# SwiGLU's Winograd products in the order P5, P6, P7, P4, P3, small gate loads on the weights' queue, half the first operands by VectorE

## The chip, the cores and the metric

One core of a Trainium2 chip runs the whole program. The metric is the device time of one execution in microseconds. Five engines work side by side, each through its own queue and in its own order: TensorE (matmul and transposes), VectorE, ScalarE, GpSimd, and SyncE, which here does nothing but issue DMAs. ScalarE issues DMAs too, between its computing instructions.

## The reference, cut to what matters

```python
h = modulate(rms_norm(x, g_pre_mix), shift, scale)      # x: 512 tokens, ctx: 256, width 2048
u, v, q, k, vv, g, d_f, d_b = split_proj(h @ w_in)      # the context too
la = log_sigmoid(d @ wd2 + bd) / 16                     # GLA's decay gates; wd2 is 16 x 512
mixed = einsum('hij,bnjhd->bnihd', w_s, layer_norm(gelu(v))) + b_s   # spatial gating
y = concatenate([u * mixed, gla_out]) @ w_out           # 1024 + 1024 columns
x = x + gate * rms_norm(y)
a, b = split(modulate(rms_norm(x), ...) @ w_ffn_in)     # 2048 -> 2 x 5632
x = x + gate2 * rms_norm((silu(a) * b) @ w_ffn_out)
```

All tensors are float32.

## The kernel before

Every float32 matmul operand is split into a high and a low part (`hi`, a rounded copy made by ScalarE, and `lo`, the rest, by VectorE), and `three` multiplies hi x hi, hi x lo and lo x hi. Names that end in h and l are such parts. Work that is not urgent comes from generators that two pumps step once per weight tile: `bg` (spatial gating, residual, operand preparation) and `bgm` (the modulation vectors).

**Context projections.** The weights of the context's keys (`ck`) and values (`cv`) come tile by tile through SyncE's queue (`ckr`, `cvr`, three buffers). TensorE multiplies them while `bg` runs the spatial gating: `wsr` is loaded, transposed (`wsp`), multiplied into `cb`, and eight heads follow, each with `mx` on TensorE, the load `ul` of the gate operand, `mt` on VectorE and the store `a_dr`, both DMAs on SyncE. `wdc` is the low-rank weight whose product `cd` runs beside `ck`; ScalarE casts it. Two tiles `wd2` for the decay gates are cleared by GpSimd and then filled by twelve DMAs of 1 KB to 16 KB (L673, L674). They are used only after the context projections.

**First operands of the FFN.** The normalised tokens are transposed by TensorE into PSUM, 256 columns at a time, and `h2_pair` scales and shifts them into `h2f` (L1141). `half` 0 serves the first two token tiles; `make_top` asks for eight pairs of it, j = 0 and 1 each. `s_parts` casts them into operands S1 and S2; S3 to S7 come later, from `make_rest`. The residual of the second half (`residual`) runs between them: a norm over VectorE and ScalarE, then new scaled rows `yo`.

**SwiGLU.** The product with `w_ffn_in` runs by 2 x 2 blocks with seven products instead of eight (Strassen-Winograd). Eleven groups of 512 hidden columns each take P1 to P7; one product is 48 matmuls of 512 columns in four quarters q. A quarter loads one 128x1024 block of weights (SyncE, four buffers `R`), sums it with the running chain `X` where the product wants a sum, and casts (`parts`): P5 adds block (0,1), P6 adds (1,1), P4 adds (1,0). After these come P3 and P7 in turn: z is block (1,1), and y is (0,1) plus z. Products leave PSUM through 128x512 sums by VectorE (`vtt`, L1202): `u`, `u4` (printed w), `a1` (printed g). [...] Groups 0 to 5 have their P1 and P2 made earlier, partly between the groups. `turn_hidden` transposes a finished group and stores it to DRAM; `hidden` loads it back (`gr`, R buffers) and casts it into `gh`, `gl` for the last projection `fo`. In the last group eight of those parts are made ahead of P7 and P3, and P3 loads its blocks again (`v`).

Of the kernel before, what the change touches and what calls it, by code (L numbers as in the profile page):

```python
# [14 lines left out]
AF = mybir.ActivationFunctionType  # L15
ALU = mybir.AluOpType
# [9 lines left out]
HID = 5632  # L26
# [67 lines left out]
def trunk_kernel(ctx, tc, cmat, cmask, x, c, ctxt, c_ctx, w_mod, b_mod, g_pre_mix, g_post_mix, g_pre_ffn,  # L94
                 g_post_ffn, w_in, ln_g, ln_b, w_s, b_s, wd2_f, bd_f, wd2_b, bd_b, out_g, w_out, w_ffn_in,
                 w_ffn_out, out):
    nc = tc.nc
    V, S, T, G = nc.vector, nc.scalar, nc.tensor, nc.gpsimd
# [12 lines left out]
    def bank(name, main=True):  # L111
        return pm.tile([P, 512], F32, tag="mm" if main else "ms", bufs=6 if main else 2, name=name)

    def slot(name, dt=F32, shape=(P, 512)):
        return s2.tile(list(shape), dt, tag="s2", bufs=NS, name=name)
# [177 lines left out]
    def pump():  # L293
        bg.step()
        bgm.step()
# [14 lines left out]
    def three(o, a, b, start, stop, lhs_first=True):  # L310

        mm(o, a[0], b[0], start, False)
        mm(o, a[0], b[1], False, False)
        mm(o, a[1], b[0], False, stop)

    def cut(pair, lo, n):
        return pair[0][:, lo:lo + n], pair[1][:, lo:lo + n]
# [35 lines left out]
    def turn(o, tok, k, diag=None):  # L353

        for i in range(len(tok)):
            src = tok[i][k // 4][:, (k % 4) * P:(k % 4 + 1) * P]
            if diag is None:
                T.transpose(o[:, i * P:(i + 1) * P], src, ident)
            else:
                mm(o[:, i * P:(i + 1) * P], src, diag[:, i, :], True, True)  # L360
# [5 lines left out]
    fmodA = cp.tile([P, KT], F32, name="fmodA")  # L366
    fmodB = cp.tile([P, KT], F32, name="fmodB")
# [139 lines left out]
    for ka, kb in ((0, 4), (4, 8), (8, KT)):  # L507
        first, last = ka == 0, kb == KT
# [154 lines left out]
    bgm.drain()  # L663


    wd2 = [slot(f"wd2{g}") for g in range(2)]
    for g in range(2):
        G.memset(wd2[g][:65, :], 0.0)
        w4 = wd2[g].rearrange("p (h d c) -> p h d c", h=2, d=2)
        for d_, (w, b_) in enumerate(((wd2_f, bd_f), (wd2_b, bd_b))):  # L670
            src = w[0][:, g * 256:(g + 1) * 256].rearrange("r (h c) -> r h c", h=2)
            for r in (0, 32):
                nc.scalar.dma_start(w4[r + 16 * d_:r + 16 * d_ + 16, :, d_, :], src)  # L673
            nc.scalar.dma_start(w4[64:65, :, d_, :],  # L674
                                b_[0:1, g * 256:(g + 1) * 256].rearrange("r (h c) -> r h c", h=2))


    def mods_ffn_in():
        for k0 in range(0, KT, 4):
            yield from mod_ab(3 * D, k0, 4, cx, gpf, fmodA, fmodB, "mf", mod_bg, late=1)  # L680
# [18 lines left out]
    def turn_ck(i):  # L699

        ps = bank(f"ckx{i}", False)
        for j in range(2):
            h = 2 * i + j
            for t in range(NC):
                T.transpose(ps[:, j * CTX + t * P:j * CTX + (t + 1) * P], ckt[t][:, h * P:(h + 1) * P], ident)
        S.copy(ckT[i], ps)

    cvacc = [[bank(f"cv{t}_{g}") for g in range(2)] for t in range(NC)]
    for k, ws in stream(w_in[0], OVV, 1024, KT, "cv"):
# [17 lines left out]
    for o in (0, 512):  # L727
        n = min(512, len(LEVELS) * P - o)
# [290 lines left out]
    def raw2(name):  # L1019
        return st2.tile([P, 1024], F32, tag="R", bufs=4, name=name)  # L1020

    def parts(src, name):

        wh = st2.tile([P, 1024], F32R, tag="wh", bufs=3, name=name + "h")
        wl = st2.tile([P, 1024], F32R, tag="wl", bufs=3, name=name + "l")
        S.copy(wh, src)
        V.tensor_tensor(out=wl, in0=src, in1=wh.bitcast(F32), op=ALU.subtract)
        return wh, wl

    def wide(w, r, c0, t, name):  # L1030

        load(t.rearrange("p (k c) -> p k c", k=2), w[r:r + 2 * P, c0:c0 + 512].rearrange("(k p) c -> p k c", p=P))
        return t
# [90 lines left out]
    NQ = KT // 4  # L1124
# [8 lines left out]
    def h2_pair(half, k0):  # L1133

        ps = bank(f"h2p{half}_{k0}", False)
        tmp = slot(f"h2f{half}_{k0}")
        for j in range(2):
            k = k0 + j
            c = slice(j * 256, (j + 1) * 256)
            turn(ps[:, c], yo[half * 2:half * 2 + 2], k)  # L1140
            S.activation(tmp[:, c], ps[:, c], AF.Identity, bias=fmodB[:, k:k + 1], scale=fmodA[:, k:k + 1])  # L1141
        return tmp

    top = [[None] * NQ for _ in range(2)]
# [41 lines left out]
    def product(p, q, accs, wp, nq):  # L1186
        hi, lo = SP[p][q]
        for j in range(2):
            for t in range(2):
                c = slice(j * 256 + t * P, j * 256 + (t + 1) * P)  # L1190
                three(accs[t], (hi[:, c], lo[:, c]), cut(wp, j * 512, 512), q == 0 and j == 0, q == nq - 1 and j == 1)

    def two(name):
        return [bank(f"{name}{t}") for t in range(2)]
# [5 lines left out]
    def vtt(out, a, b, op):  # L1200
        for i in range(2):
            V.tensor_tensor(out=out[i], in0=a[i], in1=b[i], op=op)  # L1202

    def blk(gi, i, j, q, t):

        return wide(w_ffn_in[0], i * (D // 2) + 2 * q * P, (gi * 512, HID + gi * 512)[j], t, f"f{gi}")
# [30 lines left out]
    def hidden(k0, nk):  # L1237

        for k in range(k0, k0 + nk, 2):
            r = raw2(f"gr{k}")  # L1240
            nc.sync.dma_start(r.rearrange("p (k c) -> p k c", k=2), g_dr[k:k + 2].rearrange("k p c -> p k c"))
            for j in range(2):
                hi, lo = slot(f"gh{k + j}", F32R), slot(f"gl{k + j}", F32R)
                S.copy(hi, r[:, j * 512:(j + 1) * 512])  # L1244
                V.tensor_tensor(out=lo, in0=r[:, j * 512:(j + 1) * 512], in1=hi.bitcast(F32), op=ALU.subtract)  # L1245
                yield (hi, lo)
# [22 lines left out]
    gT, src = [], hidden(0, 20)  # L1269

    def ffn_group(gi):
        n = f"f{gi}"
        if gi not in early:
            u, X = ffn_top(gi, chain_tile)
            a1 = ffn_top2(gi, u)
        else:
            X = [blk(gi, 0, 0, q, chain_tile(f"{n}X{q}")) for q in range(NQ)]
            u, a1 = early[gi] if gi < 2 else (kept(gi, 0, "r"), kept(gi, 2, "r"))

        p5 = two(n + "p5")  # L1280
        for q in range(NQ):
            r = blk(gi, 0, 1, q, raw2(f"{n}c{q}"))
            V.tensor_tensor(out=X[q], in0=X[q], in1=r, op=ALU.add)
            product(5, q, p5, parts(X[q], f"{n}c{q}"), NQ)
            pump()
        turn_hidden()
        p6 = two(n + "p6")
        for q in range(NQ):
            r = blk(gi, 1, 1, q, raw2(f"{n}d{q}"))
            V.tensor_tensor(out=X[q], in0=X[q], in1=r, op=ALU.add)  # L1290
            product(6, q, p6, parts(X[q], f"{n}d{q}"), NQ)
            pump()
        vtt(u, u, p6, ALU.subtract)
        u4 = [fslot(f"{n}w{t}") for t in range(2)]
        vtt(u4, p5, u, ALU.add)
        p4 = two(n + "p4")
        for q in range(NQ):
            r = blk(gi, 1, 0, q, raw2(f"{n}e{q}"))
            V.tensor_tensor(out=X[q], in0=X[q], in1=r, op=ALU.add)
            product(4, q, p4, parts(X[q], f"{n}e{q}"), NQ)  # L1300
            pump()
        vtt(u, p4, u, ALU.add)
        if gi == HID // 512 - 1:
            for _ in range(8):
                gT.append(next(src))

        p7, p3 = two(n + "p7"), two(n + "p3")
        last = gi == HID // 512 - 1
        for q in range(NQ):
            z = blk(gi, 1, 1, q, raw2(f"{n}z{q}"))  # L1310
            y = blk(gi, 0, 1, q, raw2(f"{n}y{q}"))
            if not last:
                product(3, q, p3, parts(z, f"{n}z{q}"), NQ)
                pump()
            V.tensor_tensor(out=y, in0=y, in1=z, op=ALU.add)
            product(7, q, p7, parts(y, f"{n}y{q}"), NQ)
        vtt(u, u, p7, ALU.subtract)
        for t in range(2):
            S.activation(u[t], u[t], AF.Silu)
        vtt(p7, p7, u4, ALU.subtract)  # L1320
        if last:
            vtt(u, u, p7, ALU.mult)
            for q in range(NQ):
                z = blk(gi, 1, 1, q, raw2(f"{n}v{q}"))
                product(3, q, p3, parts(z, f"{n}v{q}"), NQ)
                pump()
        vtt(u4, p3, u4, ALU.subtract)
        vtt(a1, a1, u4, ALU.mult)
        if not last:
            vtt(u, u, p7, ALU.mult)  # L1330
        behind.append((gi, a1 + u))

    behind = []
# [45 lines left out]
    for ci, (k1, nk) in enumerate(((0, 20), (20, 20))):  # L1379
        if ci:  # L1380
            gT, src = [], hidden(k1, nk)
# [22 lines left out]
    gT = list(hidden(HID // P - LAST, LAST))  # L1404
# [4 lines left out]
    for t in range(NT):  # L1409
# [5 lines left out]
        for cg in range(4):  # L1415
            ps = bank(f"fz{t}{cg}")
            for k in range(LAST):
                three(ps, cut(gT[k], t * P, P), wl_[cg * LAST + k], k == 0, k == LAST - 1)
            f = facc[t][cg]
# [4 lines left out]
        r = rstd_exp(fss, 1, f"er{t}")  # L1424
# [32 lines left out]
```

## Time and profile before

| | |
|---|---|
| median of three runs | 2322.54 us (2322.45, 2322.54, 2324.78) |
| the profiled execution | 2318.14 us, of which the span 2314.9 us |
| granted TensorE clock over the span | 0.993 |
| TensorE busy | 2251.0 us, 97% |
| VectorE busy | 1597.7 us, 69% |
| ScalarE busy | 986.8 us, 43% |
| DMA traffic | 496.16 MB, 214 GB/s over the span |

The profile is of one execution. Its time is the span of the engines' records and 3.2 us around it. Busy times say how much of the span an engine worked, not which engine the others waited for; the rows further down come from single stretches of the trace. The granted clock is a share of 2.4 GHz.

### The profile page before, as it was taken

Reading aid. Unit: us, or ns where it says so; the run is one execution under the profiler, and the core shown is the slowest. Engines: PE = TensorE matmul, PEld = TensorE weight load, DVE = VectorE, ACT = ScalarE, POOL = GpSimd, SP = SyncE. Lnnn points to the kernel's source line nnn. Section 1 sums busy time; section 2 is a strip of 40 time slices with the busy share of each in tenths; the row PEclk is TensorE's granted clock in tenths of the full one; section 3 lists DMA queues with packets and bytes.
Section 4 is the critical chain, followed back from the end, with each engine's and each line's share of the span. In section 5 each row is a group of like instructions: output and inputs, shape, how many; then the busy total and the mean of one; then the engine's idle time right before and its main releaser. Section 6 shows DMA issues by size and latency. Waiting matters only on the chain.

```text
span 2314.9 us, 27795 instructions
## 1 busy us (share of the span) xinstructions
PE 2251.0 (97%) x10298; PEld 1829.1 (79%) x10298; DVE 1597.7 (69%) x2072; ACT 986.8 (43%) x1517; POOL 15.5 (1%) x25
## 2 busy tenths in 40 slices
PE   7999998999999999999999999999999999999998
PEld 2778887888878777777888788888888788888886
DVE  3886586687796565797878887788788643354346
ACT  4444334465564325864444444444445322241232
POOL 0000000000000000000000000000000000000000
PEclk9999999999999999999999999999999999999999
DMA  9966787854462686777687776676566754464344
GB/s 322 338 221 223 244 294 243 298 178 128 146 198 87 231 276 237 227 221 246 215 282 263 264 256 198 191 225 195 183 215 207 243 191 146 139 228 161 122 135 157
DMA packets 262391, 496.16 MB, mean 214 GB/s; under 512 B 22128, under 2 KB 33872, under 8 KB 262256
## 3 DMA queue, kind: packets, MB, share of 16 engines
q1 hardware_dynamic: 248960, 472.47, 62.5%
q10 hardware_dynamic: 13296, 21.94, 2.7%
q8 instruction: 80, 1.31, 0.2%
q14 instruction: 55, 0.45, 0.1%
HBM read 466.01 MB, written 28.32 MB: 214 GB/s over the span
## 4 chain that ended last, share of the span: by engine, by line
PE 76%; DMA 10%; DVE 9%; ACT 3%; issue 2%; SPq 0%; ACTq 0%; DVEq 0%
PE fo L118 16%; PE wo L118 3%; PE f8p L118 3%; PE f1p L118 3%; PE f7p L118 3%; PE f9p L118 3%; PE f6p L118 3%; PE f5p L118 3%; PE f3p L118 2%; PE f0p L118 2%; PE f4p L118 2%; PE vv1a L118 2%; PE v0a L118 2%; PE u1a L118 2%; PE fz L118 2%; PE cv L118 2%
## 5 line engine op out<-in xcount | busy, mean ns | idle before, releaser
L1245 DVE TENSOR_TENSOR gl<-gr,gh 128x512 fp32r<-128x512 f32 x44 | 28.9, 688 | 26.5 <-ACT gh L1244 26.4
L1244 ACT CAST gh<-gr 128x512 fp32r<-128x512 f32 x44 | 25.3, 618 | 47.9 <-DMA gr<-g_dr 41.0
L229 DVE SCALAR_TENSOR_TENSOR m53acc<-m53w,cpair,m53acc 128x512 f32<-128x512 f32 x16 | 12.0, 750 | 28.5 <-DMA m53w<-in_w_mod_dram 28.5
L229 DVE SCALAR_TENSOR_TENSOR m21acc<-m21w,cpair,m21acc 128x1024 f32<-128x1024 f32 x16 | 20.5, 1283 | 14.7 <-DMA m21w<-in_w_mod_dram 14.7
L862 ACT ACTIVATE lv<-lv 128x1024 f32<-128x1024 f32 x20 | 21.0, 1056 | 22.5 <-DVE lv L861 22.5
L229 DVE SCALAR_TENSOR_TENSOR m20acc<-m20w,cpair,m20acc 128x1024 f32<-128x1024 f32 x16 | 20.5, 1283 | 12.8 <-DMA m20w<-in_w_mod_dram 12.6
L118 PE MATMUL g1a<-hxh,g_0h 128*128 128x512 f32 x64 | 27.1, 423 | 0.3 <-ACT g_0h L289 0.3
L1421 ACT ACTIVATE junk<-fc 128x512 bf16<-128x512 f32 x16 | 10.1, 631 | 40.4 <-DVE fc L1420 40.3
L118 PEld LDWEIGHTS s<-lv 128*128 128x128 f32 x192 | 25.0, 191 | 2.7 <-PE g1a L118 0.7
L118 PE MATMUL vv0a<-vv_0h,hxh 128*128 128x512 f32 x64 | 26.8, 419 | 0.0
L118 PE MATMUL g0a<-hxh,g_0h 128*128 128x512 f32 x64 | 26.8, 419 | 0.0
L118 PE MATMUL vv1a<-vv_0h,hxh 128*128 128x512 f32 x64 | 26.3, 426 | 0.0
L118 PE MATMUL v1a<-v_0h,hxh 128*128 128x512 f32 x64 | 26.3, 411 | 0.0
L229 DVE SCALAR_TENSOR_TENSOR mc4acc<-mc4w,cpair,mc4acc 128x1024 f32<-128x1024 f32 x16 | 20.5, 1284 | 8.3 <-DMA mc4w<-in_w_mod_dram 8.1
L118 PE MATMUL fo<-fo_0h,gh 128*128 128x512 f32 x64 | 25.4, 397 | 0.6 <-DVE fc L1400 0.6
L118 PE MATMUL v1a<-v_0l,hxh 128*128 128x512 f32 x64 | 26.0, 406 | 0.0
L118 PE MATMUL s<-lv 128*128 128x128 f32 x192 | 25.6, 275 | 0.3 <-DVE lv L863 0.3
L118 PE MATMUL g0a<-hxh,g_0l 128*128 128x512 f32 x64 | 25.8, 403 | 0.0
L118 PE MATMUL fo<-fo_12h,gh 128*128 128x512 f32 x64 | 25.7, 402 | 0.0
L118 PE MATMUL v1a<-v_0h,hxl 128*128 128x512 f32 x64 | 25.6, 400 | 0.0
L118 PE MATMUL vv0a<-vv_0l,hxh 128*128 128x512 f32 x64 | 25.5, 399 | 0.0
L118 PE MATMUL vv1a<-vv_0l,hxh 128*128 128x512 f32 x64 | 25.4, 397 | 0.0
(3919 smaller groups left out, 7841.8 us busy)
## 6 DMA issues: line engine op xcount, KB each, us to landing
fo_r<-in_w_ffn_out_dram SPq DMA_DIRECT2D x80, 512.0 KB
gr<-g_dr SPq DMA_DIRECT2D x22, 512.0 KB
mx4w<-in_w_mod_dram SPq DMA_DIRECT2D x16, 512.0 KB
mx8w<-in_w_mod_dram SPq DMA_DIRECT2D x16, 512.0 KB
mx12w<-in_w_mod_dram SPq DMA_DIRECT2D x16, 512.0 KB
mc4w<-in_w_mod_dram SPq DMA_DIRECT2D x16, 512.0 KB
mc8w<-in_w_mod_dram SPq DMA_DIRECT2D x16, 512.0 KB
mc12w<-in_w_mod_dram SPq DMA_DIRECT2D x16, 512.0 KB
```

The costliest lines, as they stand in the source:

```text
L118: return T.matmul(o, lhsT=l, rhs=r, start=start, stop=stop)
L229: ins = V.scalar_tensor_tensor(out=acc, in0=raw[:, j].rearrange("p i c -> p (i c)"), scalar=cvec[:, k0 + j:k0 + j + 1], in1=acc, op0=ALU.m ...
L862: S.activation(lv, lv, AF.Exp)
L1244: S.copy(hi, r[:, j * 512:(j + 1) * 512])
L1245: V.tensor_tensor(out=lo, in0=r[:, j * 512:(j + 1) * 512], in1=hi.bitcast(F32), op=ALU.subtract)
L1421: S.activation(junk, f, AF.Square, accum_out=fss[:, cg:cg + 1])
```

## The change

There are three edits. The twelve wd2 loads move from ScalarE's queue, ahead of the context projections, to SyncE's queue, behind `ck`'s loop. In `h2_pair`, VectorE does the scaling of j = 1 for half 0. In `ffn_group`, P7 follows P6 and takes X minus a fresh load of block (0,0), then P4, and P3 comes last with no sum; the second SwiGLU factor's last subtraction comes after P3. In the last group, four gT parts (two gr loads) are asked for in P3's quarters in place of eight ahead of P7.

```diff
-    wd2 = [slot(f"wd2{g}") for g in range(2)]
-                nc.scalar.dma_start(w4[r + 16 * d_:r + 16 * d_ + 16, :, d_, :], src)
-            nc.scalar.dma_start(w4[64:65, :, d_, :],
+    wd2 = [slot(f"wd2{g}") for g in range(2)]
+                nc.sync.dma_start(w4[r + 16 * d_:r + 16 * d_ + 16, :, d_, :], src)
+            nc.sync.dma_start(w4[64:65, :, d_, :],
...
-            S.activation(tmp[:, c], ps[:, c], AF.Identity, bias=fmodB[:, k:k + 1], scale=fmodA[:, k:k + 1])
+            if j and not half:
+                V.tensor_scalar(out=tmp[:, c], in0=ps[:, c], scalar1=fmodA[:, k:k + 1], scalar2=fmodB[:, k:k + 1],
+                                op0=ALU.mult, op1=ALU.add)
+            else:
+                S.activation(tmp[:, c], ps[:, c], AF.Identity, bias=fmodB[:, k:k + 1], scale=fmodA[:, k:k + 1])
...
         vtt(u4, p5, u, ALU.add)
+        p7 = two(n + "p7")
+        for q in range(NQ):
+            r = blk(gi, 0, 0, q, raw2(f"{n}y{q}"))
+            V.tensor_tensor(out=r, in0=X[q], in1=r, op=ALU.subtract)
+            product(7, q, p7, parts(r, f"{n}y{q}"), NQ)
+            pump()
+        vtt(u, u, p7, ALU.subtract)
+        vtt(p7, p7, u4, ALU.subtract)
         p4 = two(n + "p4")
...
         vtt(u, p4, u, ALU.add)
-        if gi == HID // 512 - 1:
-            for _ in range(8):
-                gT.append(next(src))
-
-        p7, p3 = two(n + "p7"), two(n + "p3")
...
         for t in range(2):
             S.activation(u[t], u[t], AF.Silu)
...
+        vtt(u, u, p7, ALU.mult)
+        p3 = two(n + "p3")
+        for q in range(NQ):
+            product(3, q, p3, parts(blk(gi, 1, 1, q, raw2(f"{n}z{q}")), f"{n}z{q}"), NQ)
+            pump()
+            if gi == HID // 512 - 1:
+                gT.append(next(src))
         vtt(u4, p3, u4, ALU.subtract)
         vtt(a1, a1, u4, ALU.mult)
-        if not last:
-            vtt(u, u, p7, ALU.mult)
```

ScalarE's instructions at the start of the context's key projection, before (`hch` is a cast of the context's normalised columns, `lnb`, `bsr` and `wsr` are loads of the spatial gating):

```order
L565 CAST hch_3102<-xcT_3095 128x512
L673 DMA wd_3106<-in_gla_wd_fwd_dram 16x2x128 x2
L674 DMA wd_3106<-in_gla_bd_fwd_dram 1x2x128
L673 DMA wd_3106<-in_gla_wd_bwd_dram 16x2x128 x2
L674 DMA wd_3106<-in_gla_bd_bwd_dram 1x2x128
L673 DMA wd_3107<-in_gla_wd_fwd_dram 16x2x128 x2
L674 DMA wd_3107<-in_gla_bd_fwd_dram 1x2x128
L673 DMA wd_3107<-in_gla_wd_bwd_dram 16x2x128 x2
L674 DMA wd_3107<-in_gla_bd_bwd_dram 1x2x128
L385 CAST wdc_3134<-wdcr 128x8x32
L224 DMA mf0acc<-in_b_mod_dram 1x2x512
L602 DMA lnb_3169<-in_gmlp_ln_b_dram 128x512
```

and after:

```order
L565 CAST hch_3102<-xcT_3095 128x512
L385 CAST wdc_3118<-wdcr 128x8x32
L224 DMA mf0acc<-in_b_mod_dram 1x2x512
L602 DMA lnb_3153<-in_gmlp_ln_b_dram 128x512
L604 DMA bsr_3155<-in_gmlp_bs_dram 1x512
L606 DMA wsr_3157<-in_gmlp_ws_dram 128x4x128
```

The twelve loads no longer stand between the cast of `hch` and that of `wdc`.

SyncE's queue at the first value tiles, before:

```order
L205 DMA mf0w_3556<-in_w_mod_dram 128x2x512
L197 DMA cvr_3559<-in_w_in_dram 128x1024
L197 DMA cvr_3581<-in_w_in_dram 128x1024
L652 DMA a_dr<-mt_3487 128x512
L645 DMA ul_3550<-u_dr 128x512
L205 DMA mf0w_3614<-in_w_mod_dram 128x2x512
L197 DMA cvr_3617<-in_w_in_dram 128x1024
L205 DMA mf0w_3645<-in_w_mod_dram 128x2x512
L652 DMA a_dr<-mt_3552 128x512
L645 DMA ul_3608<-u_dr 128x512
L197 DMA cvr_3648<-in_w_in_dram 128x1024
```

and after:

```order
L197 DMA cvr_3559<-in_w_in_dram 128x1024
L704 DMA wd_3481<-in_gla_wd_fwd_dram 16x2x128 x2
L652 DMA a_dr<-mt_3471 128x512
L705 DMA wd_3481<-in_gla_bd_fwd_dram 1x2x128
L704 DMA wd_3481<-in_gla_wd_bwd_dram 16x2x128 x2
L705 DMA wd_3481<-in_gla_bd_bwd_dram 1x2x128
L704 DMA wd_3482<-in_gla_wd_fwd_dram 16x2x128 x2
L705 DMA wd_3482<-in_gla_bd_fwd_dram 1x2x128
L704 DMA wd_3482<-in_gla_wd_bwd_dram 16x2x128 x2
L705 DMA wd_3482<-in_gla_bd_bwd_dram 1x2x128
L645 DMA ul_3550<-u_dr 128x512
L197 DMA cvr_3581<-in_w_in_dram 128x1024
```

The twelve loads now lie between the third value tile, cvr_3559, and the fourth, cvr_3581; a store a_dr and a load ul have also gone ahead of the fourth.

VectorE at the end of group 1, where `f4X` and `f2X` belong to the work that follows, before:

```order
L1027 TENSOR_TENSOR f4a1l<-f4X_9589,f4a1h 128x1024
L1202 TENSOR_TENSOR f1u_8163<-f1u_8163,f1p_9405 128x512
L1202 TENSOR_TENSOR f1u_8164<-f1u_8164,f1p_9406 128x512
L1202 TENSOR_TENSOR f1p_9405<-f1p_9405,f1w_9321 128x512
L1202 TENSOR_TENSOR f1p_9406<-f1p_9406,f1w_9322 128x512
L1202 TENSOR_TENSOR f1w_9321<-f1p_9407,f1w_9321 128x512
L1202 TENSOR_TENSOR f1w_9322<-f1p_9408,f1w_9322 128x512
L1202 TENSOR_TENSOR f1g_8281<-f1g_8281,f1w_9321 128x512
L1202 TENSOR_TENSOR f1g_8282<-f1g_8282,f1w_9322 128x512
L1202 TENSOR_TENSOR f1u_8163<-f1u_8163,f1p_9405 128x512
L1202 TENSOR_TENSOR f1u_8164<-f1u_8164,f1p_9406 128x512
L1027 TENSOR_TENSOR f4a2l<-f4X_9607,f4a2h 128x1024
```

and after:

```order
L1206 TENSOR_TENSOR f1u_8163<-f1u_8163,f1p_9325 128x512
L1206 TENSOR_TENSOR f1u_8164<-f1u_8164,f1p_9326 128x512
L1027 TENSOR_TENSOR f1z3l<-f1z_9547,f1z3h 128x1024
L1027 TENSOR_TENSOR f4a0l<-f4X_9571,f4a0h 128x1024
L1027 TENSOR_TENSOR f4a1l<-f4X_9589,f4a1h 128x1024
L1206 TENSOR_TENSOR f1w_9321<-f1p_9491,f1w_9321 128x512
L1206 TENSOR_TENSOR f1w_9322<-f1p_9492,f1w_9322 128x512
L1206 TENSOR_TENSOR f1g_8281<-f1g_8281,f1w_9321 128x512
L1206 TENSOR_TENSOR f1g_8282<-f1g_8282,f1w_9322 128x512
L1027 TENSOR_TENSOR f4a2l<-f4X_9607,f4a2h 128x1024
L1287 TENSOR_TENSOR f2X_9681<-f2X_9681,f2c_9699 128x1024
L1027 TENSOR_TENSOR f4a3l<-f4X_9625,f4a3h 128x1024
```

Five pairs of sums stood together behind `f4a1l`; now two pairs stand there, and the other three come further ahead, among the operands of P4 and P3.

## Rows read from the trace of the kernel before

**Rows 1.** The profile's first part: busy time and share of the span, by engine.

```profile
PE 2251.0 (97%) x10298; PEld 1829.1 (79%) x10298; DVE 1597.7 (69%) x2072; ACT 986.8 (43%) x1517; POOL 15.5 (1%) x25
```

**Rows 2.** Chain that ended last, 360 to 420 us: start, duration (us), what.

```profile
364.43 3.79 DMA ckr<-in_w_in_dram
...
369.19 1.55 DMA wd<-in_gla_wd_bwd_dram
...
372.20 6.00 DMA wsr<-in_gmlp_ws_dram
...
398.32 2.94 PE ck L118 x12
...
402.15 5.46 PE cv L118 x24
```

**Rows 3.** Timeline of ScalarE with its DMA issues (ACTq), 362 to 374 us.

```profile
363.78 0.35 ACTq L673 DMA_DIRECT2D wd<-in_gla_wd_fwd_dram  x1
...
370.12 0.57 ACTq L674 DMA_DIRECT2D wd<-in_gla_bd_bwd_dram  x1
```

**Rows 4.** Waits of TensorE, 364 to 386 us: us in total, times, longest.

```profile
PE wsp L627 <- DMA wsr<-in_gmlp_ws_dram: 4.7, 1, 4.7
PE cd L118 <- DVE wdc L386: 2.6, 1, 2.6
```

**Rows 5.** Windows: busy (instructions) of PE, PEld, DVE, ACT, POOL, clock, DMA share, GB/s.

```profile
380.00:385.00 5.00, 5.00 (x15) 3.89 (x14) 3.89 (x6) 1.28 (x3) 0.00 (x0) 0.61 0.93 302
385.00:390.00 5.00, 5.00 (x23) 4.14 (x23) 4.58 (x6) 3.97 (x9) 0.00 (x0) 1.00 1.02 377
```

**Rows 6.** Timeline of SyncE's queue (SPq) and TensorE, 393 to 419 us.

```profile
393.88 6.72 SPq L197 DMA_DIRECT2D cvr<-in_w_in_dram  x2
...
411.07 0.39 PE L118 MATMUL cv<-cv_0h,hch 128*128 128x512 f32 x1
```

**Rows 7.** Waits of TensorE, 936 to 962 us.

```profile
PE f0p L118 <- ACT f0a2h L1026: 1.9, 1, 1.9
PE f0p L118 <- ACT f0b0h L1026: 1.2, 1, 1.2
PE f1p L118 <- ACT f1a0h L1026: 1.1, 1, 1.1
```

**Rows 8.** Windows, columns as in group 5.

```profile
940.00:945.00 5.00, 4.75 (x14) 3.84 (x15) 5.00 (x9) 0.30 (x2) 0.00 (x0) 0.66 0.72 228
```

**Rows 9.** Lines by form: ScalarE, 915 to 962 us; VectorE, 340 to 420.

```profile
L1141 ACT ACTIVATE h2f<-h2p,fmodB,fmodA 128x256 f32<-128x256 f32 x16 | 8.3, 570 | 0.1
...
L697 DVE COPY dcT<-cd 64x256 f32<-64x256 f32 x1 | 0.4, 415 | 2.1 <-PE cd L118 2.1
```

**Rows 10.** Timeline of SyncE's queue, group 10 of the FFN.

```profile
1770.30 8.22 SPq L1241 DMA_DIRECT2D gr<-g_dr  x4
```

**Rows 11.** Waits of TensorE, 1790 to 1806 us.

```profile
PE f10p L118 <- DVE f10y1l L1027: 2.7, 1, 2.7
PE f10p L118 <- ACT f10y1h L1026: 1.0, 1, 1.0
```

**Rows 12.** Windows, columns as in group 5.

```profile
1800.00:1805.00 5.00, 4.71 (x14) 3.72 (x15) 2.69 (x3) 1.05 (x2) 0.00 (x0) 0.66 0.89 295
```

**Rows 13.** Timeline of VectorE in group 1 of the FFN, 1100 to 1152 us.

```profile
1115.47 1.22 DVE L1027 TENSOR_TENSOR f1e2l<-f1X,f1e2h 128x1024 fp32r<-128x1024 f32 x1
1116.61 1.22 DVE L1315 TENSOR_TENSOR f1y<-f1y,f1z 128x1024 f32<-128x1024 f32 x1
...
1145.43 1.28 DVE L1202 TENSOR_TENSOR f1u<-f1u,f1p 128x512 f32<-128x512 f32 x2
...
1151.42 1.22 DVE L1027 TENSOR_TENSOR f4a2l<-f4X,f4a2h 128x1024 fp32r<-128x1024 f32 x1
```

**Rows 14.** Waits of TensorE, 1025 to 1092 us.

```profile
PE f1p L118 <- DVE f1c0l L1027: 2.2, 1, 2.2
PE f0p L118 <- DVE f0c2l L1027: 1.1, 1, 1.1
```

More of the change, by code (lines that the diff above doesn't have):

```diff
@@ L663, in trunk_kernel @@
     bgm.drain()
-    wd2 = [slot(f"wd2{g}") for g in range(2)]
[L667 to L672, printed above, removed]
-                nc.scalar.dma_start(w4[r + 16 * d_:r + 16 * d_ + 16, :, d_, :], src)
-            nc.scalar.dma_start(w4[64:65, :, d_, :],
-                                b_[0:1, g * 256:(g + 1) * 256].rearrange("r (h c) -> r h c", h=2))
     def mods_ffn_in():
@@ L706, in turn_ck @@
         S.copy(ckT[i], ps)
+    wd2 = [slot(f"wd2{g}") for g in range(2)]
+    for g in range(2):
+        G.memset(wd2[g][:65, :], 0.0)
+        w4 = wd2[g].rearrange("p (h d c) -> p h d c", h=2, d=2)
+        for d_, (w, b_) in enumerate(((wd2_f, bd_f), (wd2_b, bd_b))):
+            src = w[0][:, g * 256:(g + 1) * 256].rearrange("r (h c) -> r h c", h=2)
+            for r in (0, 32):
+                nc.sync.dma_start(w4[r + 16 * d_:r + 16 * d_ + 16, :, d_, :], src)
+            nc.sync.dma_start(w4[64:65, :, d_, :],
+                                b_[0:1, g * 256:(g + 1) * 256].rearrange("r (h c) -> r h c", h=2))
     cvacc = [[bank(f"cv{t}_{g}") for g in range(2)] for t in range(NC)]
@@ L1302, in ffn_group @@
         vtt(u, p4, u, ALU.add)
-        if gi == HID // 512 - 1:
-            for _ in range(8):
-                gT.append(next(src))
-        p7, p3 = two(n + "p7"), two(n + "p3")
[L1308 to L1311, printed above, removed]
-            if not last:
[L1313 to L1317, printed above, removed]
         for t in range(2):
             S.activation(u[t], u[t], AF.Silu)
-        vtt(p7, p7, u4, ALU.subtract)
-        if last:
-            vtt(u, u, p7, ALU.mult)
[L1323 to L1326, printed above, removed]
+        vtt(u, u, p7, ALU.mult)
[5 more added lines that the diff above has]
+                gT.append(next(src))
         vtt(u4, p3, u4, ALU.subtract)
         vtt(a1, a1, u4, ALU.mult)
-        if not last:
-            vtt(u, u, p7, ALU.mult)
         behind.append((gi, a1 + u))
```

## Prediction

> **What bounds the kernel now.** I read the profile's first part, then TensorE's waits, then the places where those waits are long. TensorE is busy for 2251.0 us, 97% of the span [rows 1], so the kernel is bound by its matmuls, whose number the change leaves alone. Only what TensorE loses can be won: waits, and the slower clock that follows a long one. For the matmuls I use one price: 24 matmuls of 512 columns took 5.46 us, 0.2275 us each [rows 2]; the 48 of one SwiGLU product make 10.9 us. The change touches three places, and I cost each from its own stretch.
>
> **A, the small loads.** Before, ScalarE's queue holds the twelve wd loads in front of the second wdc cast and the wsr load. The first issues at 363.78, the last at 370.12 for 0.57 us, so they fill 6.9 us [rows 3]. The chain that ended last runs through them: a ckr load (3.79 us), the last wd load (1.55), then wsr, issued at 372.20 and 6.00 us in landing [rows 2]. TensorE waits 2.6 us for wdc and 4.7 us for wsr [rows 4]. Afterwards its clock is 0.61 on average, a mixture of 1.2 and 2.4 GHz, and it starts 15 matmuls in 5 us where the next 5 us at full clock hold 23 [rows 5]: eight missing, 8 x 0.2275 = 1.8 us. The loss is 2.6 + 4.7 + 1.8 = 9.1 us.
>
> After, cast and wsr come forward by about 6 us (the 6.9, less some 0.9 in which ScalarE casts hch anyway, an estimate). If wsr again takes 6.00 us it lands near 372.2. TensorE wanted it at 378.2 - 4.7 = 373.5 and, with the wait for wdc gone, wants it at 370.9. About 1.3 us of wait stay, which I take as too short for the clock to fall; if it falls, up to 1.8 us come back. **Gain 7.8 us.**
>
> The twelve loads now stand in SyncE's queue between the third and the fourth cv tile; with them a_dr and ul change places. The first waits for the clearing of its tile, which waits for the cb matmuls that last used the slot. Those end at 398.32 before [rows 2], so at 390.5 after. The program hands its DMAs eight semaphores in turn, so that an issue waits for the landing of the DMA eight places ahead (in the chain above, a wd issue follows the ckr load's landing); the last wd loads so wait for the first. On ScalarE's queue the issues took 0.35 to 0.57 us [rows 3]; at 0.46 twelve cost 5.5 us. a_dr, which stands behind the first two of them, needs mt, which needs the first mx matmuls (they end at 402.15 [rows 2], so at 394.4) and two VectorE operations of about 0.7 us: 396. Ten wd issues and ul behind it bring the fourth cv tile to about 401.4, where before it was issued at the end of 393.88 + 6.72 = 400.6 [rows 6]. So the load is no earlier, while TensorE is 7.8 us earlier. With a landing like ckr's 3.79 us [rows 2] and 1.3 us of casts, its matmuls can start at 406.5. Before they started at 411.07 [rows 6], which is 403.3 on the new clock: a stall of 3.2 us. The next two tiles come through the same a_dr, ul, cvr chain; I add 1.3 us for them. **Cost 4.5 us, A = -3.3.** Bounds: with no stall -7.8; with wsr's 6.00 us for every landing on that chain (2.2 more for the wd loads, for cvr, and twice for ul and cvr of the next tiles, and a slow clock of 1.8 again), about 10 more, A = +7.
>
> The row says 6.9 us of issues in front of a cast and a load that TensorE waits for [rows 3, 4]. The Trainium skill speaks against part A: "DMA: Bandwidth & Descriptors", section "Issuing engines are not separate DMA queues", says all issuers share the same 16 DMA engines, so another issuer saves only the sequencer's issuing time, usually small beside the transfer. By it the gain of 7.8 would be near nothing and the cost would stay. This trace disagrees: 6.9 us stood on the queue against 1.55 us of transfer. I take the row.
>
> **B, the first operands.** ScalarE's h2f activations from PSUM cost 0.57 us each [rows 9]; eight of sixteen go. TensorE waits 1.9 us for f0a2h and 1.2 us for f0b0h [rows 7], both casts queued behind them on ScalarE, then runs at an average clock of 0.66: 14 matmuls in 5 us against 23, less the 0.25 us of wait inside, 1.8 us [rows 8, 5]. Together 4.9 us. Without eight activations (8 x 0.57 = 4.6 us, of which about 4 are start to start) the casts come forward by about 4 and the waits go. VectorE takes the eight: the nearest row is a copy of 64x256 out of PSUM, 0.415 us [rows 9], so 3.3 us; VectorE is not the waited-for engine there. Not all of 4.9 is kept: f1a0h, which already costs 1.1 us [rows 7], hangs on the norm of the second token half (residual), a chain over VectorE that does not move as far. I give back 1.9. **B = -3** (bounds: 0, if that chain stands still, and -5).
>
> **C, the order of products.** VectorE's work is the same in number: 36 operations of 128x1024 and 16 of 128x512 per group. What moves is where they stand.
> - *Last group.* Before, four gr loads hold the R buffers (issues 1770.30 for 8.22 us [rows 10]), so the f10z and f10y loads are late; TensorE waits 2.7 and 1.0 us [rows 11], then starts 14 matmuls in 5 us at a clock of 0.66 [rows 12]: 9 x 0.2275, less 0.3 of wait, 1.7. Of 5.4 us I expect 5 back: two gr loads go between the z loads during P3, the four reloads of block (1,1) are not made twice, and P7 needs one loaded tile per quarter. With half as many gh/gl ready, the first fo matmuls may wait up to 1 us. **-4.5.**
> - *End of each group.* Before, five pairs of 128x512 operations run from 1145.43 to 1151.42 [rows 13], 1.2 us a pair, ahead of the next group's operands. TensorE's waits for those operands include 2.2 us for f1c0l and 1.1 us for f0c2l [rows 14]; shorter ones of later groups are left out of the sum. After, two pairs stand there (2.4 us), 3.6 us less, more than either wait: **-3.3.**
> - *New load on VectorE.* In P7 and P4 alike, eight operations of 1.14 us start to start [rows 13] and two pairs of 1.2 us make 11.5 us against TensorE's 10.9. Before, P4 alone was so. Each such stage loses 0.6 us if VectorE has no lead; over 22 stages 13 us. P5 and P6 (9.1 against 10.9) build a lead of about 3.6, so I put **+1.0.**
> - *Loads.* e, y and z take an R buffer from issue to cast: 3.8 of landing plus three operations of about 1.1 make 7 us, under the 10.9 us that four buffers allow. Nothing.
>
> **C = -6.8**, bounds -8.7 (all of 5.4 and 3.3, nothing new) and +5.2 (no lead at all, 13 against the 7.8).
>
> **Sum.** -3.3 - 3 - 6.8 = -13.1. The profiled execution took 2318.1, so 2305 for one like it. The median of the runs shown, 2322.5, lies 4.4 above it; I forecast on the median: 2322.5 - 13.1, rounded, 2309.
>
> **The rivals.**
> - *The cv tiles eat part A.* The fourth to sixth cv tiles stall for 7.8 us or more. For it: three more steps in front of cvr, and SyncE's queue is in order. Against it: landings of 1.55 and 3.79 us. Result with A = 0: 2322.5 - 9.8, about 2313, and with A = +7, 2320.
> - *The issuer does not matter (the page's rule as a mechanism here).* wdc and wsr then wait for the 16 engines rather than for the queue: the wsr wait stays 4.7 us, only the queue's cost remains, A about +4.5, result 2317. Against it: the 6.9 us on ScalarE's queue [rows 3].
> - *VectorE bounds P7 and P4.* C becomes +5.2; result 2322.5 - 3.3 - 3 + 5.2 = 2321, the same within measurement. For it: the price of 11.5 against 10.9 rests on rows; against it: the lead from P5 and P6.
> - *Slower.* One mechanism: the landing time of the small loads and of what follows them on SyncE's queue. Each microsecond more for every landing costs about 4 us of A (wd, cvr, then ul and cvr again). To lose B's and C's 9.8 and 4.6 more, A has to reach +14.4, 17.7 above my value, which needs landings of 8.2 us; at 8.5 us about 2328. For it: wsr took 6.00 [rows 2] while 16 engines were 0.93 busy [rows 5]. Against it: 3.79.
> - *More.* No cv stall and all the waits of B and C gone: 2322.5 - 7.8 - 5 - 8.7 = 2301, less the shorter waits that I left out.
>
> **How the numbers follow.** Forecast (2303 to 2315) 0.56; cv tiles eat A 0.13; issuer rule 0.05; VectorE bound 0.12; slower 0.06; more 0.08. A measurement of this kernel tells a difference of about 0.2%, 4.6 us, from none: faster is below 2317.9, slower above 2327.1. Faster: 0.56 from the forecast, 0.11 of the eaten A, 0.03 of the issuer rule (its 2317 lies at the edge), 0.02 of VectorE's, 0.08 of more: 0.80; slower: the rival's 0.06 and 0.02 for the bad ends of the others; same 0.12. The range leaves out the slower rival, VectorE's end above 2320 and the far end of more: 2299 to 2320.
>
> **What would show it.** A right: no wait for wdc, one of about 1.3 us for wsr, no window below full clock near 380, and new waits of cv for cvr of 3 to 6 us near 395 to 410. B right: no waits for f0a2h and f0b0h, f1a0h's wait longer. C right: no f10y waits, f1c0l's wait gone; wrong, if waits for the l halves of y and e (VectorE) of 0.3 us or more stand in nearly every group. The prediction is wrong if the cv waits exceed 8 us or VectorE's waits in P7 and P4 exceed 9 us in all.

## The result and the profile after

The changed kernel took 2353.52 us in the median of four runs (2344.91 to 2359.36), the kernel before 2322.49 (2319.28 to 2324.78): ratio 1.014, 95% interval 1.0121 to 1.0159; by the ratio that is 32 us slower. The forecast was 2309, faster. The profiled execution is the slowest of the four, 2359.36 us, so its trace shows somewhat more loss than the median does.

The profile's first part, with the span and the busy time of each engine; it answers to [rows 1]:

```profile
span 2357.2 us, 27770 instructions
...
PE 2267.7 (96%) x10298; PEld 1841.1 (78%) x10298; DVE 1602.8 (68%) x2080; ACT 981.9 (42%) x1509; POOL 15.5 (1%) x25
```

The span is 42.3 us longer. TensorE is busy for 16.7 us more with the same 10298 matmuls, and the other 25.6 us are idle. The granted clock over the span fell from 0.993 to 0.985; 0.8% of the span is 19 us, about what the busy time grew by. The waits show where it falls. TensorE's waits over the whole execution (us in total, times, longest):

```profile
PE f3p L118 <- DVE f3c3l L1027: 4.0, 1, 4.0
PE f10p L118 <- DVE f10b2l L1027: 4.0, 1, 4.0
...
PE cv L118 <- ACT cv_0h L289: 3.6, 1, 3.6
PE f1p L118 <- DVE f1c3l L1027: 3.6, 1, 3.6
PE fo L118 <- DVE gl L1249: 3.6, 1, 3.6
PE f5p L118 <- DVE f5c3l L1027: 3.3, 1, 3.3
PE f2p L118 <- ACT f2c2h L1026: 3.2, 1, 3.2
PE f6p L118 <- DVE f6b2l L1027: 2.8, 1, 2.8
PE f7p L118 <- DVE f7b2l L1027: 2.7, 1, 2.7
...
PE f8p L118 <- DVE f8b2l L1027: 2.2, 1, 2.2
PE f4p L118 <- ACT f4c2h L1026: 2.1, 1, 2.1
...
PE f9p L118 <- DVE f9b2l L1027: 1.5, 1, 1.5
...
PE wsp L627 <- DMA wsr<-in_gmlp_ws_dram: 0.9, 1, 0.9
```

The waits for wdc, f0a2h, f0b0h and all of f10y are gone [rows 4, 7, 11]. New, or longer, are ten waits of 1.5 to 4.0 us, one in each of the groups 1 to 10, for parts named c (P5) or b (P2); the ten rows add up to 29.4 us. Only the one for f6b2l was there before, with 1.0 us. There is none for y or e, where P7 and P4 were feared to be bound by VectorE.

What stands ahead of such a part on VectorE? The timeline of VectorE in group 1, where TensorE waits 3.6 us for f1c3l (start, duration in us, line, operation, and in brackets the idle time before it and what ended it):

```profile
1090.33 1.22 DVE L1027 TENSOR_TENSOR f1c2l<-f1X,f1c2h 128x1024 fp32r<-128x1024 f32 x1
1091.46 3.49 DVE L1294 TENSOR_TENSOR f1X<-f1X,f1d 128x1024 f32<-128x1024 f32 x3
1097.77 1.23 DVE L1303 TENSOR_TENSOR f1y<-f1X,f1y 128x1024 f32<-128x1024 f32 x1 [2.81 <-DMA f1y<-in_w_ffn_in_dram]
1100.69 1.22 DVE L1303 TENSOR_TENSOR f1y<-f1X,f1y 128x1024 f32<-128x1024 f32 x1 [1.70 <-DMA f1y<-in_w_ffn_in_dram]
1101.83 1.22 DVE L1027 TENSOR_TENSOR f1c3l<-f1X,f1c3h 128x1024 fp32r<-128x1024 f32 x1
```

and of ScalarE, the cast that f1c3l needs:

```profile
1094.73 1.05 ACT L1026 CAST f1c3h<-f1X 128x1024 fp32r<-128x1024 f32 x1 [1.00 <-ACT f0t L1340]
```

From 1095.8, when its cast ends, f1c3l could have run. But in VectorE's queue two subtractions of the new P7, f1y<-f1X,f1y, stand ahead of it, and each waits for its f1y load (2.81 and 1.70 us). VectorE takes its instructions in order, so f1c3l starts at 1101.83, 6 us after its cast, and TensorE stands. Groups 3 and 5 show the same, with waits of VectorE of 6.5 and 5.1 us for a y load. The y operands themselves are wanted only after the whole of P6.

In groups 6 to 10 the blocking instruction is another one, the third sum of P5. VectorE in group 7, before:

```profile
1508.51 1.22 DVE L1027 TENSOR_TENSOR f7b0l<-f7b,f7b0h 128x1024 fp32r<-128x1024 f32 x1
...
1517.76 1.22 DVE L1027 TENSOR_TENSOR f7b2l<-f7b,f7b2h 128x1024 fp32r<-128x1024 f32 x1
...
1520.67 1.23 DVE L1283 TENSOR_TENSOR f7X<-f7X,f7c 128x1024 f32<-128x1024 f32 x1 [0.55 <-DMA f7c<-in_w_ffn_in_dram]
```

and after:

```profile
1533.04 1.22 DVE L1027 TENSOR_TENSOR f7b0l<-f7b,f7b0h 128x1024 fp32r<-128x1024 f32 x1 [1.49 <-ACT f7b0h L1026]
...
1545.71 1.23 DVE L1287 TENSOR_TENSOR f7X<-f7X,f7c 128x1024 f32<-128x1024 f32 x1 [3.88 <-DMA f7c<-in_w_ffn_in_dram]
1546.85 1.22 DVE L1027 TENSOR_TENSOR f7b2l<-f7b,f7b2h 128x1024 fp32r<-128x1024 f32 x1
```

The third f7c load is as late in one as in the other: its sum starts 12.2 us after f7b0l before and 12.7 after. Before, f7b2l stood ahead of this sum and ran 9.3 us after f7b0l. After, it stands behind it and runs at 13.8. Nothing in this line was changed; the scheduler that orders VectorE's queue placed the sums anew. That it did so because the products around them moved is my reading and not shown.

Two of the ten waits, for f2c2h and f4c2h, have another engine behind them: they are casts, and ScalarE's own queue holds them. ScalarE in group 2, after:

```profile
1167.62 0.81 ACTq L1341 DMA_DIRECT2D g_dr<-f1t  x2
1170.20 0.33 ACTq L1271 DMA_DIRECT2D early_dr<-f4u  x1
1170.57 1.04 ACT L1026 CAST f2c2h<-f2X 128x1024 fp32r<-128x1024 f32 x1 [5.69 <-DMA g_dr<-f1t]
```

and the chain that ended last at that place:

```profile
1162.67 7.50 DMA g_dr<-f1t
```

The store early_dr stands ahead of the cast and goes out at 1170.20, just after an earlier store, g_dr, has landed at 1170.17; ScalarE is idle for 5.69 us in front of the cast.

A wait is not the whole price. The windows of the changed kernel around this place (columns as in [rows 5]):

```profile
1545.00:1550.00 5.00, 2.26 (x7) 1.51 (x6) 4.29 (x4) 1.01 (x1) 0.00 (x0) 0.74 0.65 215
1550.00:1555.00 5.00, 5.00 (x15) 3.95 (x14) 2.61 (x3) 1.04 (x1) 0.00 (x0) 0.57 0.93 319
```

Behind the wait the granted clock is 0.57 of 2.4 GHz, mostly the level of 1.2 GHz, and TensorE starts 15 matmuls in 5 us where a window at full clock holds 23 [rows 5]: 8 x 0.2275 = 1.8 us on top of the 2.7.

### The profile page after: what moved, and what is told of

Same layout as the page of the kernel before. It is cut to its first block, busy times and chain, and to the rows that moved or that the text cites. A ratio compares the mean times of both kernels' runs of the same rounds, so it can differ in the third digit from the quotient of the medians.

```text
span 2357.2 us, 27770 instructions
## 1 busy us (share of the span) xinstructions
PE 2267.7 (96%) x10298; PEld 1841.1 (78%) x10298; DVE 1602.8 (68%) x2080; ACT 981.9 (42%) x1509; POOL 15.5 (1%) x25
## 4 chain that ended last, share of the span: by engine, by line
PE 75%; DMA 12%; DVE 8%; ACT 2%; issue 2%; SPq 0%; ACTq 0%; DVEq 0%
PE fo L118 16%; PE wo L118 3%; PE f9p L118 3%; PE f6p L118 3%; PE f8p L118 3%; PE f1p L118 3%; PE f7p L118 3%; PE f10p L118 3%; PE f2p L118 3%; PE f5p L118 2%; PE f4p L118 2%; PE f0p L118 2%; PE f3p L118 2%; PE k L118 2%; PE vv1a L118 2%
## 5 line engine op out<-in xcount | busy, mean ns | idle before, releaser
L118 PE MATMUL fo<-fo_4h,gl 128*128 128x512 f32 x64 | 25.4, 399 | 3.6 <-DVE gl L1249 3.6
L118 PE MATMUL s<-lv 128*128 128x128 f32 x192 | 25.6, 275 | 0.1
L118 PE MATMUL fo<-fo_6h,gh 128*128 128x512 f32 x64 | 25.6, 400 | 0.0
```

The source lines that it names most:

```text
L118: return T.matmul(o, lhsT=l, rhs=r, start=start, stop=stop)
```

## The experiments

All ratios are against the kernel before on the same chip; a difference of 0.001 in the ratio is 2.3 us, and the microseconds given are those of the ratio. The theory: VectorE's in-order queue holds a sum that waits for its load in front of a part that TensorE needs. The rivals: the loads are late for lack of R buffers, whatever the order; VectorE has too much work in P7 and P4; the three parts disturb each other.

**One part at a time.** Each of the first three kernels has one of the edits as it stands in the change's diff.

> Only part A, the twelve small loads on SyncE's queue. The trace of the full change shows the waits for wdc gone, wsr at 0.9 us, and new waits of cv for its tiles of 3.6 and 0.7 us. Theory (the cv tiles eat the gain): within 3 us of the kernel before. The prediction's own value was -3.3 us. If the small loads carry a good part of the loss, it is slower by 8 us or more.

Measured: 2318.86 us, ratio 0.9995 (0.9979 to 1.0011). No difference that can be told.

> Only part B, eight of the h2f scalings by VectorE. Theory (the casts f0a2h and f0b0h come forward and nothing else moves): faster by 3 to 5 us. If VectorE's extra work delays what follows, no change or slower by a few us.

Measured: 2316.28 us, ratio 0.9971 (0.9958 to 0.9984), 6.7 us faster (3.7 to 9.8). The waits for f0a2h and f0b0h are gone, one of 1.2 us for f0b1l is new, and that for the first part of f1a, 1.1 before, is 0.3.

> Only part C, the order of the products and the last group. Theory (the whole loss is here, at the start of each group, where VectorE's queue holds a sum that waits for its load ahead of a part that TensorE needs): slower by 30 to 38 us. If the loss comes from the three parts together (the queues and the DMA traffic of the others), slower by 20 us or less.

Measured: 2359.53 us, ratio 1.0165 (1.0139 to 1.0191), 38 us slower. Added, -1 - 7 + 38 = 30, beside 32 for the whole: within the intervals the parts add, and the loss lies in the order of the products.

**The order on VectorE's queue.** The same work in part C, with one rule more: a sum of a loaded block may not stand ahead of the low part of the block two before its own.

```diff
-        V.tensor_tensor(out=wl, in0=src, in1=wh.bitcast(F32), op=ALU.subtract)                # in parts()
+        lows.append(V.tensor_tensor(out=wl, in0=src, in1=wh.bitcast(F32), op=ALU.subtract).ins)
...
+    def after_low(back, **kw):
+        with tc.issue_after(lows[-back]):     # order of issue only
+            V.tensor_tensor(**kw)
...
-            V.tensor_tensor(out=X[q], in0=X[q], in1=r, op=ALU.add)          # c, d, e
+            after_low(2, out=X[q], in0=X[q], in1=r, op=ALU.add)
-            V.tensor_tensor(out=r, in0=X[q], in1=r, op=ALU.subtract)        # y
+            after_low(2, out=r, in0=X[q], in1=r, op=ALU.subtract)
```

> Part C alone, with the same work, but each sum of a loaded block (X plus c, d, e and X minus y) stands on VectorE's queue no earlier than behind the low part two quarters ahead of its own. Theory of the queue: the waits of 2 to 4 us for c2, c3 and b2 go, and with them the loss: faster than before by 4 to 10 us. Rival (the loads land late because the R buffers come free later, whatever the order on VectorE): still slower by 20 us or more. Second rival (VectorE has 11.5 us of work in P7 and P4 against TensorE's 10.9): slower by 5 to 13 us, with small waits in P7 and P4 of nearly every group.

Measured: 2318.3 us, ratio 0.9988 (0.9974 to 1.0002). The 38 us are gone, and neither rival's time came. What is left, 3 us faster (6 faster to 0.5 slower), can't be told from no change and is less than the 4 to 10 us expected. The waits for c3 and b2 are gone, one of 2.1 us for f4c2h stays. VectorE at the same place in group 1 of this kernel:

```profile
1091.93 1.23 DVE L1027 TENSOR_TENSOR f1c3l<-f1X,f1c3h 128x1024 fp32r<-128x1024 f32 x1 [2.95 <-ACT f1c3h L1026]
...
1100.43 1.22 DVE L1034 TENSOR_TENSOR f1y<-f1X,f1y 128x1024 f32<-128x1024 f32 x1
```

f1c3l now starts as soon as its cast allows, and f1y stands 8.5 us behind it and waits for nothing.

> Part C alone with only the new subtraction X minus y held; the sums with c, d, e stand where the scheduler puts them. Theory of the queue: the waits for c2 and c3 at the start of P5 in groups 1 to 5 go, those for b2 in groups 6 to 10 stay: slower than before by 12 to 22 us. If the subtraction of y is the whole cause: no slower than 3 us.

```diff
+            after_low(2, out=r, in0=X[q], in1=r, op=ALU.subtract)           # y alone; c, d, e as in part C
```

Measured: 2343.89 us, ratio 1.0088 (1.0067 to 1.0109), 20 us slower. TensorE's waits of this kernel:

```profile
PE f9p L118 <- DVE f9b2l L1027: 3.4, 1, 3.4
PE f6p L118 <- DVE f6b2l L1027: 3.2, 1, 3.2
...
PE f2p L118 <- ACT f2c2h L1026: 2.4, 1, 2.4
```

f1c3l, f3c3l and f5c3l have left the list, the waits for b2 of groups 6 to 10 have stayed (2.6 to 3.4 us). So each of the two kinds of sum carries about half of the loss. Against what I expected, the waits for f2c2h and f4c2h stay too (2.4 and 2.0 us); they are those of ScalarE's queue.

**Is it the hold itself, or the late loads?** The kernel before with its sums held in the same way:

> The kernel before, old order of products, with its sums X plus c, d, e held in the same way (y plus z is left free). If holding the sums is a gain by itself, faster by 3 us or more, and the new order then adds nothing. If the hold only takes back what the new order brought, within 2 us of the kernel before.

Measured: 2319.13 us, ratio 0.9995 (0.9983 to 1.0007). The hold gains nothing by itself; it takes back what the new order brought. And part C, sums free, with a fifth R buffer:

```diff
-NF = 29
+NF = 27
-        return st2.tile([P, 1024], F32, tag="R", bufs=4, name=name)
+        return st2.tile([P, 1024], F32, tag="R", bufs=5, name=name)
```

> Part C alone, sums not held, with five R buffers in place of four (paid for by two of 29 buffers f), so that loads can go out one buffer earlier. Rival theory (the loads are late for lack of buffers): most of the loss goes, within 10 us of the kernel before. Theory of the queue: the subtractions of y still stand ahead of c3's low part, and the scheduler moves sums further ahead with the room it has: still slower by 15 us or more, with DMA waits of VectorE at y or c.

Measured: 2327.5 us, ratio 1.0031 (1.0022 to 1.0041), 7 us slower. Here my theory missed: I had expected 15 or more, and the rival's forecast, within 10 us, came true. VectorE's waits in this kernel:

```profile
DVE f3y L1299 <- DMA f3y<-in_w_ffn_in_dram: 5.5, 1, 5.5
...
DVE f1y L1299 <- DMA f1y<-in_w_ffn_in_dram: 3.8, 1, 3.8
DVE f5y L1299 <- DMA f5y<-in_w_ffn_in_dram: 3.8, 1, 3.8
```

and TensorE's:

```profile
PE f3p L118 <- DVE f3c3l L1027: 4.2, 1, 4.2
...
PE f1p L118 <- DVE f1c3l L1027: 3.4, 1, 3.4
```

In groups 1 to 5 the subtractions of y still wait ahead of c3 and TensorE with them. In groups 6 to 10 the waits for b2 are gone, though the sums stand even further ahead there. VectorE still waits for an f6c to f10c load, but for 1.9 us at most, where the changed kernel has 2.7 to 5.0 in each of these groups. The stages of the profiled executions show both halves. They are in us by the starts of TensorE's first matmuls with f1c0h, f6a0h and f10c0h, of the first fo, and by the end of the span:

| kernel | groups 1 to 5, from P5 of group 1 | groups 6 to 10, up to P5 of group 10 | rest of group 10 | last projection |
|---|---|---|---|---|
| before | 332.1 | 338.7 | 61.1 | 494.3 |
| the whole change | 354.4 | 359.4 | 54.4 | 500.1 |
| the order alone | 352.5 | 356.9 | 54.4 | 500.4 |
| the order, y held | 335.7 | 362.4 | 54.4 | 503.4 |
| the order, all sums held | 334.7 | 337.5 | 54.5 | 500.2 |
| the order, five buffers | 352.0 | 337.0 | 54.4 | 493.4 |

The hold of y mends the first column alone, the fifth buffer the second alone, and the hold of all sums both. So the late loads of the rival are a cause in groups 6 to 10, and in groups 1 to 5 a fifth buffer does not help: 20 us are still there. The kernel is only 7 us slower because it also keeps the 6.7 us won in the rest of group 10 without the price in the last projection that the others pay. A sum in front costs when its load is late by more than the lead of the part behind it: place and lateness are both needed; the theory had only the place. That the two f buffers taken away cost nothing is not shown.

**Small loads and the whole change, mended.**

> The full change (small loads, first operands, order) with the sums held as in the run of the order alone. If the three parts add, -3.5, -6.1 and -4.1 us of the three medians make it faster by 10 to 14 us, near 2310. If the gains of the parts overlap, faster by 6 us or less.

Measured: 2317.37 us, ratio 0.9982 (0.997 to 0.9994), 4 us faster (1 to 7). The parts mended should have given 10 to 14. TensorE still waits 3.4 us for cv and 4.0 us for a gl part.

> The full change with the sums held, and the twelve small loads issued on SyncE's queue behind the last cv tile in place of between the third and the fourth. Theory (the place on SyncE's queue costs the cv stalls of about 5 us): faster than the full change with sums held by 4 to 6 us. Rival (the cv tiles are late for another reason, such as the store a_dr and the load ul ahead of them): the same within 2 us.

```diff
+    wd2 = [slot(f"wd2{g}") for g in range(2)]     # this block, on nc.sync, now stands here:
     cv = [[slot(f"cvv{t}_{g}") for g in range(2)] for t in range(NC)]   # behind the loop over cv tiles
```

Measured: 2311.23 us, ratio 0.9959 (0.9945 to 0.9973), by the ratios 5 us better than the kernel with the loads among the cv tiles, as expected. TensorE's waits from 395 to 460 us:

```profile
PE vv0a L118 <- DVE vv_0l L290: 0.9, 1, 0.9
PE la_1z L118 <- DVE la L750: 0.2, 1, 0.2
```

No cv is left among them.

> The full change with the sums held and the small loads behind the last cv tile, and in the last group two gT parts per quarter of P3 (eight in all, four gr loads) in place of one. Theory (fo waits 3.7 us for a gl part because only four are made ahead and VectorE then stands at a modulation sum that waits for its load): the wait goes with its slow clock, faster than the same kernel with four parts by 4 to 6 us, near 2306. Rival (the four more gr loads take R buffers from z, as before from z and y): a new wait in P3 of 3 us or more, no gain.

```diff
             if gi == HID // 512 - 1:
-                gT.append(next(src))
+                gT.extend((next(src), next(src)))
```

Measured: 2306.74 us, ratio 0.9934 (0.9922 to 0.9946), the lowest median of all. The wait for gl is gone, and no new one in P3 takes its place.

> Parts A and B with the small loads behind the last cv tile, old order of the products: what the two edits are worth without the third. From the stages of the traces (6 us in the context projections, 5 to 6 at the first operands): faster than before by 9 to 13 us. If it is as fast as the repaired full change, the new order of products has no value of its own.

This kernel is the one before with the h2_pair edit and the late small loads. Measured: 2307.12 us, ratio 0.9946 (0.9933 to 0.9959). The two intervals overlap: with its faults mended the new order of the products adds nothing that can be told.

> Part C alone with its sums held and eight parts made in P3: what the new order is worth when both faults are mended. From the stages (6.6 us of group 10, about 4 of the ends of groups, 6 of fo given back): faster than before by 6 to 11 us. If the ends of the groups were no loss worth speaking of, 5 us or less.

Measured: 2316.5 us, ratio 0.9988 (0.9975 to 1.0001), less than the 6 to 11 us expected. Mended in both places, the new order of the products by itself is worth 3 us (6 faster to none).

## Why the prediction was wrong

**The failed step is "Loads" in part C, with the word "Nothing".** I asked whether the buffers give the e, y and z loads enough time, and put that at 7 us of the 10.9. I did not ask what is queued on VectorE behind a sum whose load is a little late. The new P7 subtracts from X, which is ready early, so the scheduler could place its two subtractions ahead of the last part of P5; in the old P7 the sum needed z and y, both loaded late, and what stood behind it was wanted by TensorE later still: before, VectorE waits 2.76 us for an f1y load at 1134.68 and TensorE not at all. VectorE's order of before and after shows these rows, and no time is needed to see them. The Trainium skill says that ScalarE's, VectorE's and GpSimd's queues are strictly first in, first out ("PSUM — Partial Sum Buffer", section "Engine vs sequencer instructions"). The trace agrees: f1c3l, ready at 1095.8, ran at 1101.83 behind two waiting f1y. The landing in that sum was too short as well, 3.8 us where the first f1y load took 5.1, from its issue at 1092.71 to the subtraction at 1097.77; and in groups 6 to 10, half of the loss, a fifth buffer alone mends it. None of the rivals named it. The order alone costs 38 us, and holding the sums takes 41 off that. Neither of the two signs by which the whole was to be wrong came up (4.3 us of cv waits, none for VectorE in P7 and P4): I watched other places.

**"New load on VectorE"** was put at 1.0 us with a bound of 13. The trace has no wait for a part of y or e in any group, and with the sums held TensorE has no wait worth a row from 1430 to 1735 us, most of groups 6 to 9. In that kernel the waits for f1e1l, f3e1l and f5e1l are 0.5 us each, 1.5 us in all. Otherwise the lead held, and this rival falls.

**"End of each group", -3.3 us,** rested on a wrong reading of [rows 14]. I took the 2.2 us for f1c0l to come from the five pairs of sums ahead of it. The chain that ended last in the kernel before, from 1085 to 1095 us, reads otherwise:

```profile
1082.63 6.30 DMA f1c<-in_w_ffn_in_dram
```

and on VectorE, where the last of the five pairs ended at 1081.4:

```profile
1088.96 1.23 DVE L1283 TENSOR_TENSOR f1X<-f1X,f1c 128x1024 f32<-128x1024 f32 x1 [2.98 <-DMA f1c<-in_w_ffn_in_dram]
1090.10 1.22 DVE L1027 TENSOR_TENSOR f1c0l<-f1X,f1c0h 128x1024 fp32r<-128x1024 f32 x1
```

VectorE was idle for 2.98 us, until an f1c load of 6.30 us had landed, made that sum and then f1c0l. It was the very mechanism that later cost 38 us, shown in the trace of before, and I read a wait as work. The table above bears this out: with the sums held, groups 1 to 5 take 2.6 us more than before and groups 6 to 10 take 1.2 less, so no 3.3 us lie at the ends of the groups.

**"Last group", -4.5 us.** The f10y waits went, as said, and the rest of group 10 is 6.7 us shorter, more than the 5 that I expected back. The half microsecond that I gave for fewer ready gh/gl was mis-sized: the last projection is 5.9 us longer, with a wait of TensorE of 3.6 us for a gl part. VectorE before it:

```profile
1876.52 0.75 DVE L229 SCALAR_TENSOR_TENSOR m50acc<-m50w,cpair,m50acc 128x512 f32<-128x512 f32 x1 [6.01 <-DMA m50w<-in_w_mod_dram]
1877.19 1.29 DVE L1249 TENSOR_TENSOR gl<-gr,gh 128x512 fp32r<-128x512 f32 x2
```

Again an instruction that waits for a load, here the sum of a modulation row (m50), in front of what TensorE wants. Before, VectorE waits 6.64 us for an m50 load ahead of a gl too, at 1840.66, and eight parts made ahead cover it. Twice as many parts ahead took the wait away again.

**Part A, -3.3 us,** measured -1 (-5 to +3), so the value can't be told from mine or from nothing; the mechanism is the one described. The wsr wait is 0.9 us (1.3 said) with no fall of the clock behind it, and cv waits 3.6 and 0.7 us (4.5 said with their clock). But the clock fell at another place, behind the cb matmuls, with no wait of TensorE above 0.9 us in the 20 us in front; the kernel before has the same cb matmuls and stays at 1.00 there, so why it fell is not shown. The window of the changed kernel, columns as in [rows 5]:

```profile
395.00:400.00 5.00, 5.00 (x23) 4.17 (x22) 2.16 (x5) 2.21 (x4) 0.00 (x0) 0.79 0.12 45
```

SyncE's queue (start, duration):

```profile
390.38 0.33 SPq L197 DMA_DIRECT2D cvr<-in_w_in_dram  x1
393.48 0.81 SPq L704 DMA_DIRECT2D wd<-in_gla_wd_fwd_dram  x2
400.68 0.35 SPq L652 DMA_DIRECT2D a_dr<-mt  x1
...
405.79 0.57 SPq L705 DMA_DIRECT2D wd<-in_gla_bd_bwd_dram  x1
...
406.89 1.79 SPq L197 DMA_DIRECT2D cvr<-in_w_in_dram  x1
```

The a_dr store held the queue from 394.3 to 400.68, where I had put it at 396: it waits for mx, which ended at 398.7 and not at 394.4. Of that, 3 us are the first loads of this execution, for which TensorE waited that much longer than before, and most of the rest is the slow stretch. The cv tile went out at 406.89 and not 401.4. The twelve issues took 0.8 us per pair and about 0.6 for a single one. The run with the loads behind the last cv tile shows the cost, 5 us, and that it can be had back. That the issuing engine would not matter falls by its own sign: the wsr wait did not stay at 4.7 us but went to 0.9, and the wdc wait is gone, with the same transfers. The rival came from a page of the Trainium skill, "DMA: Bandwidth & Descriptors" (section "Issuing engines are not separate DMA queues"), which says that issuing takes little time beside the transfer itself. For one DMA the issue is the smaller part here too, 0.35 to 0.57 us beside 1.55 us of landing, and I was wrong to set the 6.9 us of twelve issues against the landing of one. What TensorE waited for was twelve in a row.

**Part B, -3 us,** was right in mechanism and measured -6.7 (-3.7 to -9.8). The mis-sized term is what I gave back: 1.9 us for f1a0h. Its wait shrank from 1.1 to 0.3 us, so the residual's chain moved with the rest. The eight operations took 0.54 us each on VectorE, where I had 0.42, and no wait shows it.

The slower rival that I named (landings of 8 us on SyncE's queue) was not the cause either: the small loads alone change nothing.

What stays open: why the scheduler moved the sums; why the clock fell behind the cb matmuls; and whether the mended parts together (4 us) fall short of their sum (11), for with intervals of about 3 and 6 us the two are hardly apart.

## What to carry to other kernels

When an edit makes an instruction ready earlier, a scheduler may place it earlier on its engine's queue: go through that queue and ask of each instruction that needs a load what stands behind it, and whether another engine wants that first. Count the loads that are late today without harm, since that may be a matter of order alone. Here an order of issue mended both places, one more buffer only one of them. A wait put down to an engine's instruction is worth following one step further back, to what that engine itself waited for.

## What was not expected of the hardware

The loads of 512 KB that block VectorE take 5 to 7 us from issue to landing (f1c 6.30 us in the chain above) where the ckr load of [rows 2] took 3.79. And ten waits of 29.4 us in all stand in stages that are 22.4 and 20.7 us longer than before: with the slow clock behind it, a wait cost about half of its own length again. A store counts like a load here: ScalarE's cast stood for 5.69 us behind a store that went out only when an earlier store, of 7.50 us, had landed.
